# The recurrence's steps beside the token groups, interleaved four for three

## The chip, the cores and the metric

The kernel runs on one core of one Trainium2 chip. The metric is the device time of the program in microseconds. One execution on the chip was also taken with the hardware profiler; everything said of single instructions comes from it.

## The reference

One inference step of one decoder layer, for a prompt of 1024 positions and for 8 samples of 4 positions each, 1056 tokens in all, with 1024 features:

```
z = RMSNorm(x) @ W_in                                  # split between two head groups
h = x + [ RWKV7(z_rwkv) | MultiScalePool(z_pool) ] @ W_out
h = h + PEER(RMSNorm(h))                               # 8 heads: top 16 of 128x128 product keys, 16384 experts
h = h + (p @ W_ple) * sigmoid(RMSNorm(h) @ W_pg)
y = RMSNorm_final(h)
```

Two parts of it matter here. RWKV7 is a recurrence over the positions: a state of 64x64 for each of 8 heads goes from one position to the next, so it is done in order, here in chunks of 64 positions. PEER first projects the normalised h to queries (2048 columns), scores them against two sets of 128 keys, takes the best 16 of each, and the best 16 of their pairs; the experts so chosen are then applied.

## The kernel before

Products of 32-bit numbers are made as three matmuls of rounded halves (hi times hi, lo times hi, hi times lo: lines 677 to 679). Phase A projects x and prepares the recurrence's inputs. Then the tokens go through in four **groups** of 288, 256, 256 and 256 columns (`GROUPS`), and at the end a long dense part applies all experts to 672 of the tokens (line 1244), beside gathers for the others.

Between phase A and the dense part, three kinds of work run beside each other, each written as a Python generator that yields after each step:

- `b_stream` is the **recurrence**: 16 chunks of 64 positions (`bchunk`), up to three of them active, about 19 steps each. A chunk loads its inputs (`fdc`, line 504), makes a triangular inverse by six levels of small 64x64 matmuls (line 493) with ScalarE evacuations between them (lines 533 to 560), and then needs the state `S` of the chunk before (lines 580 to 618). Its tail normalises the output on VectorE (lines 625 to 639) and stores it to `y_d` (line 640).
- `phase_c` takes one **group** of 256 or 288 columns: it loads its part of `y_d` (line 720) and the residual `h` from `hx_d` (line 725), splits y (lines 708 and 709), applies W_out in eight blocks with a residual add each (line 739), norms, and makes 16 blocks of query projections (evacuated in line 800), whose weights come in 256 KB loads (lines 666 and 667, three buffers each). The scores of four heads' halves at a time go to `sc_d` (line 811). In between, the normed and split h is stored for the dense part; the last such store, `xl_d` (line 776), reads the tile h itself. The tile h has one buffer. The group's y needs the four chunks of 64 positions that it covers.
- `t_stream` picks the experts of the group before (`top`, `select`): score rows come from `sc_d` (line 833), then VectorE takes maxima and their places, five instructions to a score row (lines 836 to 841). For some tiles the gates are then spread by small matmuls (line 1025), built by VectorE from one-hot tiles (lines 1017 to 1019), evacuated by ScalarE (line 1026) and stored; for others GpSimd scatters them (line 965).

The program goes in **rounds** (the loop at line 1258). Round one runs group one beside chunks 5 to 7; round two runs group two beside chunks 8 to 11 and the experts of group one; round three runs group three beside chunks 12 to 15 and the experts of group two. (The first 128 tokens' experts are written ahead of round two, all at once.) Round four has no recurrence left: it runs group four beside the first blocks of the dense part. So each round's recurrence makes the y that the next round's group loads first.

`merge` sets the order in which the steps of a round are written: of the streams that still live, it takes a step of the one with the smallest share done, the number of steps taken divided by a length that was stated for the stream. The framework's scheduler then places each instruction on its engine's queue, by its own estimate of times; where several are ready, those written first go first. The queues are in order: an instruction that waits holds up all behind it on its engine. SP issues nearly all loads and stores.

The lines that state the recurrence's length and run the round:

```
    def b_len(ca, cb):
        return (cb - ca) * 19
```

Of the kernel before, what the change touches and what calls it, by code (L numbers as in the profile page):

```python
# [65 lines left out]
def body(ctx, tc, io):  # L66
# [977 lines left out]
    def b_stream(ca, cb, ahead=2):  # L1044
        while nxt[0] < cb or any(c < cb for c, _ in active):
            c = nxt[0]
            if (c < min(cb + ahead, NCH) and len(active) < NSLOT and (not active or since[0] >= STAG)
                    and not (held[0] and c % NSLOT == 1)):
                active.append((c, bchunk(c)))
                nxt[0], since[0] = c + 1, 0  # L1050
            since[0] += 1
            for a in list(active):
                try:
                    next(a[1])
                except StopIteration:
                    active.remove(a)
                yield

    def b_len(ca, cb):
        return (cb - ca) * 19  # L1060
# [6 lines left out]
    def t_stream(gi):  # L1067
        for t0, m in tiles_of(gi):
            if 0 < GROUPS[gi][0] + t0 < GB:
                yield from top(tk, GROUPS[gi][0] + t0, m)  # L1070

    def t_len(gi):
        n = 0
        for t0, m in tiles_of(gi):
            if 0 < GROUPS[gi][0] + t0 < GB:
                n += 24 + 16
        return n

    def merge(streams):
        live = [[0, n, g] for n, g in streams]  # L1080
        while live:
            s = min(live, key=lambda s: s[0] / s[1])
            try:
                next(s[2])
                s[0] += 1
            except StopIteration:
                live.remove(s)
# [164 lines left out]
    def upre():  # L1252
        for b in range(NPRE):
            ublock(b)
            yield

    CL = [0, 24, 24, 24, 24]
    for step in range(1, NG + 1):
        streams = []
        if step < NG:  # L1260
            c_ = BC[step + 2:step + 4]
            streams.append((b_len(*c_), b_stream(*c_)))
        if step == 2:
            for _ in top(tk, 0, 128):
                pass
        if 0 <= step - 2 < NG:
            streams.append((t_len(step - 2), t_stream(step - 2)))
        if 0 <= step - 1 < NG:
            streams.append((CL[step], phase_c(step - 1)))
        if step == NG:  # L1270
            for _ in streams[0][1]:
                pass
            gstack.close()
            late = ctx.enter_context(tc.tile_pool(name="late", bufs=1, side="right", reuse_waits="tile"))
            gqp = ctx.enter_context(tc.tile_pool(name="gqp", bufs=2, side="right", reuse_waits="tile"))
            streams = [streams[1], (NPRE, upre())]
        merge(streams)
        if step == NG - 1:
            nc.sync.dma_start(io["wkv_p"], S[-1])
            pbx.close()  # L1280
            dr = ctx.enter_context(tc.tile_pool(name="dr", bufs=1, side="right", reuse_waits="tile"))
            dps = ctx.enter_context(tc.tile_pool(name="dps", bufs=2, side="right", space=bass.MemoryType.PSUM, reuse_waits="tile"))
            XH, XL = xsplit()
            for k in range(KB):
                nc.sync.dma_start(XH[:, k, :].bitcast(F32), xh_d[:, k, :])
                nc.sync.dma_start(XL[:, k, :].bitcast(F32), xl_d[:, k, :])
            xs = [(XH[:, k, :], XL[:, k, :]) for k in range(KB)]
# [340 lines left out]
```

## Time and profile before

| what | value |
|---|---|
| median of 3 runs | 3213.11 us (3209.81 to 3214.63) |
| the profiled execution's own time | 3221.9 us |
| its span, first to last instruction | 3220.2 us |
| TensorE busy | 3048.1 us, 95% of the span |
| VectorE, ScalarE, GpSimd busy | 2554.8, 1058.8, 1702.7 us |
| mean granted TensorE clock | 0.972 |

The profile page gives each engine's busy time, the span in forty slices, the chain of work that ended last, and groups of instructions by source line. Further views of the same trace show any stretch: busy times by stretch, instructions in order of time, the chain of waits piece by piece. Engines are PE (TensorE; PEld its weight loads), DVE (VectorE), ACT (ScalarE), POOL (GpSimd) and SP (the queue that issues transfers). L739 is line 739 of the kernel.

### The profile page before, as it was taken

Reading aid. Unit: us, or ns where it says so; the run is one execution under the profiler, and the core shown is the slowest. Engines: PE = TensorE matmul, PEld = TensorE weight load, DVE = VectorE, ACT = ScalarE, POOL = GpSimd, SP = SyncE. Lnnn points to the kernel's source line nnn. Section 1 sums busy time; section 2 is a strip of 40 time slices with the busy share of each in tenths; the row PEclk is TensorE's granted clock in tenths of the full one; section 3 lists DMA queues with packets and bytes.
Section 4 is the critical chain, followed back from the end, with each engine's and each line's share of the span. In section 5 each row is a group of like instructions: output and inputs, shape, how many; then the busy total and the mean of one; then the engine's idle time right before and its main releaser. Section 6 shows DMA issues by size and latency. Waiting matters only on the chain.

```text
span 3220.2 us, 65859 instructions
## 1 busy us (share of the span) xinstructions
PE 3048.1 (95%) x26305; PEld 2945.9 (91%) x26305; DVE 2554.8 (79%) x5390; ACT 1058.8 (33%) x1636; POOL 1702.7 (53%) x1189
## 2 busy tenths in 40 slices
PE   8998899978888888999999999999999999999998
PEld 7887888967777788999999999999999999999998
DVE  7766445678497888988888888888888888888976
ACT  6452324433335545322222222212222212212253
POOL 5111410077887770066666656665666666666633
PEclk9999999988989899999999999999999999999999
DMA  5577457777868987389999999999999999999945
GB/s 172 155 201 184 119 165 241 264 190 167 217 143 218 332 230 244 116 316 344 326 340 353 321 339 344 330 332 357 328 323 350 332 331 340 341 329 341 332 135 185
DMA packets 462531, 863.33 MB, mean 268 GB/s; under 512 B 152848, under 2 KB 241168, under 8 KB 461840
## 3 DMA queue, kind: packets, MB, share of 16 engines
q1 hardware_dynamic: 305776, 436.32, 42.0%
q0 software_dynamic: 148128, 406.03, 37.4%
q10 hardware_dynamic: 8320, 16.78, 1.5%
q8 instruction: 206, 3.38, 0.4%
q14 instruction: 101, 0.83, 0.1%
HBM read 738.25 MB, written 120.73 MB: 267 GB/s over the span
## 4 chain that ended last, share of the span: by engine, by line
PE 78%; DVE 9%; DMA 8%; ACT 2%; issue 1%; SPq 1%; POOL 1%; ACTq 0%; DVEq 0%; POOLq 0%
PE pd L1244 59%; PE ps L493 5%; PE ps L231 3%; PE ps L677 2%; PE ps L679 2%; PE ps L678 2%; DMA scq<-sc_d 1%; DMA whi<-wc_d 1%; PE ps L1025 1%; PE ps L324 1%; DMA wlo<-wc_d 1%; PE ps L1147 1%; DMA sc_d<-scs 1%; DVE I L837 0%; DMA y_d<-yo 0%
## 5 line engine op out<-in xcount | busy, mean ns | idle before, releaser
L1364 POOL DMA_INDIRECT row<-u,idx x384 | 545.0, 1419 | 471.7 <-DMA eraw<-uT 149.1
L1364 POOL DMA_INDIRECT row<-v,idx x384 | 530.4, 1381 | 311.6 <-DVE po L1381 141.0
L1220 ACT ACTIVATE ehi<-eraw 128x1024 fp32r<-128x1024 f32 x278 | 294.8, 1060 | 1109.0 <-PE pd L1244 1038.2
L965 POOL DMA_INDIRECT gs<-gl,idx x256 | 436.2, 1704 | 258.5 <-DVE idx L958 137.9
L1244 PE MATMUL pd<-XL,ehi 128*128 128x336 f32 x2176 | 515.6, 317 | 0.0
L1244 PE MATMUL pd<-XH,elo 128*128 128x336 f32 x2176 | 514.1, 317 | 0.0
L1244 PE MATMUL pd<-XH,ehi 128*128 128x336 f32 x2176 | 510.7, 316 | 3.0 <-ACT OT L1250 2.8
L1244 PE MATMUL pd<-wh,ehi 128*128 128x336 f32 (+1 forms) x2112 | 502.9, 317 | 4.9 <-ACT wh L1314 4.7
L1244 PE MATMUL pd<-wl,ehi 128*128 128x336 f32 (+1 forms) x2112 | 503.8, 317 | 1.7 <-DVE wl L1316 1.7
L1244 PE MATMUL pd<-wh,elo 128*128 128x336 f32 (+1 forms) x2112 | 503.4, 317 | 0.0
L1381 DVE SCALAR_TENSOR_TENSOR po<-row,act,po 128x1024 f32<-128x1024 f32 x381 | 488.1, 1281 | 7.0 <-DVE act L1375 0.2
L1372 DVE SCALAR_TENSOR_TENSOR row<-row,xt 128x1024 f32<-128x1024 f32 x384 | 455.5, 1218 | 4.9 <-DMA xt<-xt_d 3.7
L1222 DVE TENSOR_TENSOR elo<-eraw,ehi 128x1024 fp32r<-128x1024 f32 x278 | 342.7, 1233 | 85.0 <-ACT ehi L1220 84.6
L1244 PEld LDWEIGHTS pd<-XH,ehi 128*128 128x128 f32 x2176 | 372.3, 189 | 3.9 <-ACT OT L1250 3.0
L1244 PEld LDWEIGHTS pd<-XH,elo 128*128 128x128 f32 x2176 | 372.6, 188 | 0.0
L1244 PEld LDWEIGHTS pd<-XL,ehi 128*128 128x128 f32 x2176 | 370.1, 188 | 0.0
L1244 PEld LDWEIGHTS pd<-wh,ehi 128*128 128x128 f32 x2112 | 362.2, 188 | 5.5 <-ACT wh L1314 5.0
L1244 PEld LDWEIGHTS pd<-wl,ehi 128*128 128x128 f32 x2112 | 362.1, 188 | 2.0 <-DVE wl L1316 2.0
L1244 PEld LDWEIGHTS pd<-wh,elo 128*128 128x128 f32 x2112 | 363.2, 188 | 0.0
L677 PE MATMUL ps<-hi,whi 128*128 128x256 f32 (+1 forms) x592 | 188.9, 320 | 45.5 <-DMA whi<-wc_d 26.8
L1324 DVE TENSOR_TENSOR OT<-pd,OT 128x672 f32<-128x672 f32 x120 | 102.8, 857 | 136.7 <-PE pd L1244 136.3
L679 PE MATMUL ps<-hi,wlo 128*128 128x256 f32 (+1 forms) x592 | 182.7, 309 | 6.6 <-DMA wlo<-wc_d 4.8
(461 smaller groups left out, 4885.3 us busy)
## 6 DMA issues: line engine op xcount, KB each, us to landing
eraw<-uT SPq DMA_DIRECT2D x128, 512.0 KB
eraw<-vP SPq DMA_DIRECT2D x128, 512.0 KB
whi<-wc_d SPq DMA_DIRECT2D x108, 256.0 KB
wlo<-wc_d SPq DMA_DIRECT2D x108, 256.0 KB
g_d<-gst SPq DMA_DIRECT2D x52, 512.0 KB
gq<-g_d SPq DMA_DIRECT2D x32, 832.0 KB
gs<-zero ACTq DMA_DIRECT2D x8, 2048.0 KB
gq<-gs SPq DMA_DIRECT2D x64, 256.0 KB
```

What stands on the lines that cost most here:

```text
L231: mm(ps[:, :XW], s[:, k, :], x[:, k, a:b], start=first, stop=last)
L493: mm(o[hs], l[hs], r[hs], start=start, stop=stop)
L677: mm(ps[:, :n], whi[:, kk, :], xhi, start=k == 0, stop=False)
L679: l = mm(ps[:, :n], wlo[:, kk, :], xhi, start=False, stop=k == K - 1)
L965: l = nc.gpsimd.indirect_dma_start(out=flat, out_offset=bass.IndirectOffsetOnAxis(ap=off[:, hh, k:k + 1], axis=0), in_=gl[:, hh, k:k + 1], ...
L1220: ACT(hi, raw, AF.Copy)
L1222: sub(lo, raw, hi.bitcast(F32), op=ALU.subtract)
L1244: mm(ps[:, a, :n], w_[:, k, :], x_[:, s:s + n], start=first, stop=last)
L1324: TT(halves(OT[db]), ps[:, :, :NH], halves(OT[db]), op=ALU.add)
L1364: nc.gpsimd.indirect_dma_start(out=r[:m], out_offset=None, in_=io[tab], in_offset=bass.IndirectOffsetOnAxis(ap=idx[:m, hh, k:k + 1], axis=0))
L1372: STT(r[:m], r[:m], 1.0, xt[:m], op0=ALU.mult, op1=ALU.mult, accum_out=pre[:m, k:k + 1])
L1381: STT(po[:m], r[:m], act[:m, k:k + 1], po[:m], op0=ALU.mult, op1=ALU.add)
```

## The change

The length that the recurrence states to `merge` is four thirds of what it was, in the three rounds that it shares with the groups:

```
         streams = []
         if step < NG:
             c_ = BC[step + 2:step + 4]
-            streams.append((b_len(*c_), b_stream(*c_)))
+            streams.append((b_len(*c_) * 4 // 3, b_stream(*c_)))
```

`merge` counts a stream's share as steps taken over the stated length. With the longer length each step of the recurrence counts three quarters as much, so four are written where three were, and the recurrence comes to its end when the other streams are at three quarters. No step is added or left out.

Three places show how the queues come out. The first is ScalarE at the border from round one to round two. L800 evacuates a query block of the old group, L708 splits y of the new one, L741 is the square after its first residual add, L810 evacuates scores, and the rest (`zp`, `yx`, `vt`, `wn`) belongs to the recurrence. Before, from after the last L800 on:

```order
L555 ACTIVATE kbT<-ps 128x512
L539 ACTIVATE zp<-ps 128x256
L560 ACTIVATE vt<-ps 128x256
L580 ACTIVATE wn<-ps 128x256
L810 ACTIVATE scs<-ps,rt 32x512
L547 ACTIVATE yx<-ps 128x512
L708 ACTIVATE hi<-gst 128x256 x4
L585 ACTIVATE zp<-ps 128x256
L539 ACTIVATE zp<-ps 128x256
L741 ACTIVATE sa<-h 128x256
```

Now, from the split on:

```order
L708 ACTIVATE hi<-gst 128x256 x4
L800 ACTIVATE q<-ps 128x288
L772 ACTIVATE xhi<-h 128x288
L585 ACTIVATE zp<-ps 128x256
L810 ACTIVATE scs<-ps,rt 128x512 x2
L539 ACTIVATE zp<-ps 128x256
L810 ACTIVATE scs<-ps,rt 32x512
L547 ACTIVATE yx<-ps 128x512
L741 ACTIVATE sa<-h 128x256
```

The split now stands ahead of the last L800, and of nine evacuations of the recurrence between the last L800 and L741 (two of them stand above the rows shown) three are left. At the border from round two to round three nine become four.

The second place is SP's queue at the same border: L640 stores the last y of the round, L720 loads y, L725 loads h, L833 loads scores. Before:

```order
L776 DMA xl_d<-h 1024x1x288
L640 DMA y_d<-yo 512x1x64
L504 DMA fdc<-fd 128x1792
L811 DMA sc_d<-scs 128x512 x2
L720 DMA gst<-y_d 128x4x256
L725 DMA h<-hx_d 128x256 x7
L833 DMA scq<-sc_d 128x512
```

Now the store and the load of y, and further down, with 24 rows of the queue between the two pieces, h:

```order
L640 DMA y_d<-yo 512x1x64
L504 DMA fdc<-fd 128x1792
L720 DMA gst<-y_d 128x4x256
L663 DMA wc_d<-whi 128x512 x2
L664 DMA wc_d<-wlo 128x512
```

```order
L776 DMA xl_d<-h 1024x1x288
L811 DMA sc_d<-scs 128x512 x2
L666 DMA whi<-wc_d 128x512
L667 DMA wlo<-wc_d 128x512
L725 DMA h<-hx_d 128x256 x2
L833 DMA scq<-sc_d 128x512 x2
```

The load of y is now ahead of the last projections' transfers, and between `xl_d` and the loads of h no wait for y is left.

The third place is VectorE in round two, just ahead of the group's eighth residual add (L739). Names with V and s hold score rows, SC and cand the pairs picked from them, and L187 is the reciprocal in a chunk's tail. Before:

```order
L840 MAX V_8132<-s_8235 128x8
L841 MAX_INDEX I_8133<-V_8132,s_8214 128x8
L943 TENSOR_REDUCE gl_7803<-oh 128x32 x2
L955 ISA ci<-ci,r_8031 128x128
L841 MAX_INDEX I_8133<-V_8132,s_8235 128x8
L839 MATCH_REPLACE s_8278<-V_8132,scq 128x128
L836 MAX V_8132<-scq 128x8 x4
L739 TENSOR_TENSOR h<-ps,h 128x256
```

Now:

```order
L891 MATCH_REPLACE cand<-SC,s_8510 128x50
L187 RECIPROCAL s_9023<-s_9023 128x4
L890 MAX_INDEX CI<-SC,s_8551 128x8
L891 MATCH_REPLACE cand<-SC,s_8551 128x50
L912 TENSOR_TENSOR gt<-SC 128x64
L739 TENSOR_TENSOR h<-ps,h 128x256
```

Before, the score rows of the tile V_8132 were still under way when the add came; now the pairs of these rows are being picked, and a chunk's tail stands among them. From the round's first residual add to its eighth, VectorE's queue held 12 starts of a score row (L836) before and holds 20 now.

More of the change, by code (lines that the diff above doesn't have):

```diff
@@ L1261, in body @@
             c_ = BC[step + 2:step + 4]
-            streams.append((b_len(*c_), b_stream(*c_)))
+            streams.append((b_len(*c_) * 4 // 3, b_stream(*c_)))
         if step == 2:
```

## The prediction, as it was put on record

> **What bounds the kernel now.** I read the busy times of the rounds first, then the chain of waits around their borders, then the two engines there in order of time. In the first two views the columns are: stretch, its length, busy us of PE, PEld, DVE, ACT and POOL (instructions in brackets), granted TensorE clock, DMA share, GB/s.
>
> ```profile
> 502.36:662.81 160.45, 150.84 (x2478) 140.67 (x2474) 98.24 (x361) 73.78 (x160) 17.16 (x11) 0.97 0.80 267
> 662.81:863.11 200.30, 162.38 (x2536) 149.70 (x2538) 140.40 (x777) 66.81 (x147) 153.88 (x97) 0.88 0.78 184
> 863.11:1069.90 206.79, 163.16 (x2282) 149.41 (x2277) 167.13 (x752) 86.78 (x160) 166.84 (x98) 0.88 0.83 201
> 1069.90:1298.00 228.10, 198.51 (x1543) 188.86 (x1542) 197.01 (x748) 121.58 (x165) 99.80 (x53) 0.90 0.88 256
> 1298.00:3079.00 1781.00, 1780.95 (x11608) 1780.88 (x11609) 1561.97 (x2212) 441.58 (x525) 1079.74 (x770) 1.00 0.90 325
> ```
>
> From 1298 us on TensorE has no gap, and the change doesn't touch that part. So the end moves only by what TensorE's idle time before 1298 loses or gains: 9.6 us in round one, 37.9 in round two, 43.6 in round three. In round one TensorE is the limit (94%). Inside rounds two and three the limit changes from slice to slice:
>
> ```profile
> 720.00:740.00 20.00, 13.51 (x181) 12.51 (x179) 19.70 (x123) 4.01 (x10) 16.96 (x11) 0.83 0.41 54
> 760.00:780.00 20.00, 17.20 (x229) 15.58 (x229) 16.64 (x93) 3.53 (x9) 16.95 (x11) 0.83 0.87 222
> 820.00:840.00 20.00, 15.87 (x260) 14.38 (x256) 10.13 (x42) 7.79 (x12) 16.95 (x11) 0.97 0.88 204
> 840.00:860.00 20.00, 19.66 (x274) 17.73 (x274) 3.82 (x16) 6.58 (x16) 16.65 (x12) 0.86 0.92 229
> 860.00:880.00 20.00, 12.80 (x198) 11.95 (x198) 9.27 (x43) 3.91 (x11) 16.65 (x12) 0.83 0.92 228
> 880.00:900.00 20.00, 14.82 (x303) 13.25 (x303) 20.00 (x136) 7.50 (x20) 16.95 (x11) 1.00 0.80 172
> 1020.00:1040.00 20.00, 16.95 (x224) 15.64 (x221) 12.83 (x38) 10.81 (x16) 16.95 (x11) 0.92 0.95 224
> ```
>
> Early in rounds two and three VectorE is full (19.70 and 20.00 of 20) and TensorE waits; late in them VectorE is light (3.82 to 12.83) and TensorE and the transfers are the limit; at the border (860 to 880) nobody is full. The chain of waits names what stands there (start, length, what):
>
> ```profile
> 653.72 9.07 DMA y_d<-yo
> 662.81 5.86 DMA gst<-y_d
> 668.68 3.69 DMA scq<-sc_d
> ...
> 857.36 5.69 DMA y_d<-yo
> 863.11 6.78 DMA gst<-y_d
> ```
>
> The last chunk of a round stores its rows of y, and the next group loads them back: 14.9 us at the first border, 12.5 at the second. In order of time on SP's queue, TensorE and VectorE (start, length, engine, line; in brackets the idle time before and what ended it):
>
> ```profile
> 653.00 0.62 SPq L776 DMA_DIRECT2D xl_d<-h  x1
> 662.81 0.57 SPq L720 DMA_DIRECT2D gst<-y_d  x1
> 663.47 0.62 SPq L725 DMA_DIRECT2D h<-hx_d  x1
> 854.61 0.53 SPq L776 DMA_DIRECT2D xl_d<-h  x1
> 863.78 0.64 SPq L725 DMA_DIRECT2D h<-hx_d  x1
> 649.24 0.29 PE L679 MATMUL ps<-hi,wlo 128*128 128x288 f32 x1
> 667.72 1.12 PE L493 MATMUL ps<-yx,ltm 64*64 64x64 f32 x16 [7.24 <-ACT yx L547]
> 870.38 0.80 PE L677 MATMUL ps<-hi,whi 128*128 128x256 f32 x2 [6.17 <-ACT hi L708]
> 676.57 0.40 DVE L739 TENSOR_TENSOR h<-ps,h 128x256 f32<-128x256 f32 x1
> 878.08 0.40 DVE L739 TENSOR_TENSOR h<-ps,h 128x256 f32<-128x256 f32 x1
> ```
>
> SP's queue is in order: until the load of y may start at 662.81, the loads of h and of the scores behind it wait too. From the group's last projection matmul (649.24) to the next group's first residual add (676.57) pass 27 us.
>
> **The change part by part.** No instruction's kind or count changes; steps change places. In the new order (shown above) y's load is issued during the projections, its split (L708) stands ahead of the last evacuation of q, and h's loads wait for something else: the store of xl_d, which reads h's only buffer.
>
> Border one. The store is issued at 653.00 and done issuing at 653.62. Its landing has no row. Near ones are 3.69 us (a small load) and 9.07 us (the store of y issued right behind it on the same busy engines); I take 6, nearer the middle since it is larger than the one and ahead of the other: 659.6. Then h's load: 0.62 to issue and the 3.69 of the score load: the first add at 663.9, 12.7 us sooner than 676.57. Against that stands what filled the wait. This view has L493, the recurrence's matmuls, alone (busy us of PE and PEld; clock; DMA), for both borders:
>
> ```profile
> 649.53:669.50 19.97, 9.40 (x252) 8.38 (x252) 0.88 1.08 303
> 852.30:870.38 18.08, 9.02 (x268) 8.23 (x268) 0.97 1.08 287
> ```
>
> ScalarE's order has nine evacuations of the recurrence in the first gap before and three now, so six ninths of 9.40, 6.3 us, go ahead into round one, where TensorE is 94% full, and are paid for in full. Net 6.4 us; with a landing of 9.07 it is 3.3, with 3.69 it is 8.7.
>
> Border two. 854.61 + 0.53 + 6 = 861.1; plus 0.64 and 3.69 is 865.5, against 878.08: 12.6 us. Nine evacuations become four, so five ninths of 9.02, 5.0 us, go ahead into slices where TensorE is busy 35.5 of 40 us: 4.4 paid. Net 8.2, between 5.1 and 10.5. Both borders: 14.6 us (8.4 to 19.2).
>
> A rule of the Trainium skill bears here: "TensorE: Matmul & The Clock Gate", the section on the HAM clock gate, says that after about 3.4 us without work the array falls to half its clock, and needs about 3.4 us of work to recover. The gaps of 7.24 and 6.17 us are long enough, so by it each costs a cold start of 1.7 us, and their going would give 3.4 us more than my sum. The trace agrees only in part: the slice 860 to 880 has 0.83, but 720 to 740 has 0.83 as well.
>
> The stages between. What runs earlier in a round meets the full VectorE. In the stage of round two that applies W_out (from the first residual add, L739, to the eighth) VectorE's order now holds 20 score rows (one L836 each) instead of 12, and one more tail of a chunk is begun. A score row costs five instructions, from this grouping (line, engine, operation, count; busy us, mean ns; idle before):
>
> ```profile
> L841 DVE FIND_INDEX8 I<-V,s 128x8 uint32<-128x128 f32 x116 | 32.3, 282 | 0.0
> L837 DVE FIND_INDEX8 I<-V,scq 128x8 uint32<-128x128 f32 x116 | 31.7, 283 | 0.0
> L839 DVE MATCH_REPLACE8 s<-V,scq 128x128 f32<-128x128 f32 x116 | 31.6, 274 | 0.0
> L840 DVE MAX8 V<-s 128x8 f32<-128x128 f32 x116 | 30.5, 280 | 0.0
> L836 DVE MAX8 V<-scq 128x8 f32<-128x128 f32 x118 | 26.8, 278 | 47.3 <-DMA scq<-sc_d 47.2
> L1017 DVE TENSOR_TENSOR ab<-iota,e 128x2048 f16<-128x2048 f16 x52 | 62.9, 1216 | 20.5 <-PE ps L1025 17.2 <-ACT e L1003 3.0
> L1018 DVE TENSOR_TENSOR ab<-ab,e 128x1024 f16<-128x1024 f16 x52 | 35.1, 680 | 0.3
> L513 DVE TENSOR_TENSOR ltm<-ps,nmt 128x768 f32<-128x768 f32 x18 | 16.3, 949 | 13.5 <-PE ps L493 13.5
> L627 DVE SCALAR_TENSOR_TENSOR zp<-s,ps 128x256 f32<-128x256 f32 x12 | 4.9, 410 | 0.2
> L1026 ACT ACTIVATE gst<-ps 128x512 f32<-128x512 f32 x104 | 104.9, 1119 | 56.7 <-PE ps L1025 56.0 <-issue 0.4
> ```
>
> That is 1.4 us; eight are 11.2, and with two L513 (1.9) and half of a chunk's tail (eight steps like L627 at 0.41, 3.3 whole) 15 us, all on the path at 19.70 of 20. The projections behind it have eight score rows fewer, where VectorE has 16.64 of 20: it gives back 83%, 12.5. Loss 2.5 us. Round three: in the first half of its projections stand two chunk tails more (6.6), one state update (0.8) and two sets of one-hot tiles for the gates (L1017 and two like L1018, 2.6 each: 5.2), 12.6 us, and its W_out stage has one tail and one update less, 4.1: 8.5 us more at a full VectorE. The second half gives it back, at 12.83 of 20, so 64%: loss 3.1. If nothing were given back both cost 23.5, if all of it nothing.
>
> Border three isn't held by y. The fourth group finds eight more of the gate evacuations done at its first residual add (72 against 64); they alternate with the projections there. At 1.12 us each (L1026) that is between nothing and 9 us; I take 3, as TensorE has other work beside it.
>
> Sum: 14.6 - 5.6 + 3 = 12 us off the profiled execution, whose own time was 3221.9 us (span 3220.2), 8.8 above the median of the runs. 3213.1 - 12 gives 3201 us.
>
> **The rivals.** *Nothing to be measured*: h's store and loads take y's place in full (landing 9 us, both borders 8.4), and the stages take 5.6: 3 us, 3210. For it: the transfers have a share of 1.08 in both gaps. For it too: the order moves the recurrence less than the words say; at the last query block of round one ScalarE has 148 of its evacuations behind it for 141 before, of some fifty in a round. Against: the store of y is ahead of that traffic now. *Slower*: VectorE in round two's W_out stage and the first half of round three's projections. If the late slices don't get shorter, because weights and TensorE set them (DMA 0.92 and 0.95), 23.5 us are added and 14.6 saved: 3222 with border three unchanged. It decides once less than 8.9 of the 23.5, 38%, is given back. For it: 20.00 of 20 there. Against: TensorE is busy 19.66 in 840 to 860, and part of that is the recurrence. *More*: all 27.4 us of the four chain pieces go, and the work that goes ahead finds idle time: with border three 3183. Against: round one has only 9.6 us idle. *The clock*: without the recurrence between them the late projections leave gaps at every wait for weights, and TensorE is granted less: 0.83 for 0.97 in the last 40 us of rounds two and three is 11 us, so 3212. That is the mechanism of the clock gate's page, turned against the change; the rows bear it out weakly, as 0.97 stands beside 15.87 us of work.
>
> **How the numbers follow.** Forecast 0.43, with its own range of 3191 to 3210 (sum with the borders' bounds and the gate term); nothing 0.13; slower 0.25; more 0.13; clock 0.06. A measurement of this kernel tells about 0.2%, 6.4 us, from no change. Faster than 3206.7 is 0.37 of the forecast's 0.43, and more: 0.50. Within: 0.06 + 0.13 + 0.06 = 0.25. Slower: 0.25. The range goes from 3178, which takes in most of *more*, to 3226, past the price of *slower*.
>
> **What would show it.** Borders right: no y_d store or y load in the chain of waits there, the first residual add 12 to 14 us behind the last projection's matmul instead of 27, and h's loads right behind xl_d. Wrong: y still waited for, or 20 us and more. Stages right: rounds two and three, from first add to first add, within 10 us of 201.5 between the two adds above; wrong if one is 15 longer with VectorE full. The clock: under 0.85 in the last 40 us of a round. The forecast fails if the stages lose more than the borders give, or if TensorE's idle time before its unbroken run hardly falls.

## The result: 0.7% slower

| | median | lowest to highest | runs |
|---|---|---|---|
| before | 3212.81 us | 3209.81 to 3214.63 | 4 |
| after | 3235.59 us | 3230.11 to 3237.35 | 4 |

The ratio is 1.0069, with a 95% interval of 1.0055 to 1.0083: slower by 0.7%, 22 us, where 3201 us had been forecast; the range ended at 3226.

The page of the changed kernel, its first part, and two slices of 20 us early in round three (stretch, length, busy us of PE, PEld, DVE, ACT and POOL with instructions in brackets, granted TensorE clock, DMA share, GB/s):

```profile
span 3235.6 us, 65871 instructions
...
PE 3045.0 (94%) x26305; PEld 2943.6 (91%) x26305; DVE 2552.5 (79%) x5390; ACT 1056.4 (33%) x1634; POOL 1712.8 (53%) x1189
...
900.00:920.00 20.00, 13.68 (x252) 12.86 (x252) 20.00 (x129) 9.74 (x23) 16.66 (x12) 0.66 0.40 55
920.00:940.00 20.00, 10.60 (x88) 9.57 (x86) 19.80 (x107) 3.54 (x9) 17.26 (x10) 0.74 0.51 110
```

TensorE, VectorE and ScalarE have no more work than before. What grew is the time in which TensorE does nothing: early in round three, while VectorE is full, and at the end of round four. In the same slices of the kernel before TensorE was busy 16.93 and 16.17 us and VectorE 20.00 and 17.07.

At the two borders the queues do what was foretold. SP's queue and the first residual adds after the change, in order of time (start, length, engine, line; in brackets the idle time before and what ended it):

```profile
662.25 0.53 SPq L776 DMA_DIRECT2D xl_d<-h  x1
671.44 1.14 SPq L725 DMA_DIRECT2D h<-hx_d  x2
674.37 0.81 DVE L739 TENSOR_TENSOR h<-ps,h 128x256 f32<-128x256 f32 x2 [3.56 <-DMA h<-hx_d]
861.55 0.54 SPq L776 DMA_DIRECT2D xl_d<-h  x1
868.19 4.17 SPq L725 DMA_DIRECT2D h<-hx_d  x7
872.66 0.76 DVE L739 TENSOR_TENSOR h<-ps,h 128x256 f32<-128x256 f32 x2 [2.72 <-DMA h<-hx_d]
```

The load of y isn't among them any more; h's loads stand right behind the store of xl_d. To see where the time went instead, I cut both traces at the same events: the first residual add of each group (L739), the last projection evacuation of a group (L800), in round two also the last residual add, in round three also the fourth projection evacuation, and the 90 us behind the fourth group's last. Same columns, before:

```profile
517.71:649.57 131.86, 127.01 (x1897) 118.27 (x1896) 88.83 (x331) 62.65 (x134) 4.52 (x3) 0.97 0.78 271
649.57:676.57 27.00, 17.84 (x340) 16.08 (x340) 9.13 (x38) 7.81 (x18) 20.55 (x14) 0.87 1.02 276
676.57:709.99 33.42, 24.81 (x432) 23.14 (x432) 31.30 (x188) 12.02 (x27) 25.91 (x16) 0.88 0.75 170
709.99:853.41 143.42, 120.96 (x1776) 111.41 (x1778) 101.99 (x556) 46.48 (x101) 110.62 (x69) 0.88 0.75 174
853.41:878.08 24.67, 17.73 (x332) 16.37 (x332) 8.62 (x34) 7.15 (x17) 20.43 (x14) 0.86 1.00 253
878.08:948.72 70.64, 58.10 (x911) 53.14 (x913) 67.68 (x406) 25.31 (x62) 59.34 (x38) 0.86 0.67 136
948.72:1102.51 153.79, 122.87 (x1474) 111.48 (x1473) 118.63 (x354) 79.11 (x115) 118.36 (x65) 0.86 0.96 259
1102.51:1260.00 157.49, 144.02 (x1194) 138.84 (x1191) 141.21 (x614) 87.76 (x121) 76.42 (x41) 0.96 0.85 233
1260.00:1350.00 90.00, 80.12 (x490) 79.06 (x491) 80.40 (x393) 27.54 (x36) 0.00 (x0) 0.94 0.52 168
```

and after:

```profile
518.47:659.96 141.49, 133.53 (x2102) 124.65 (x2101) 91.06 (x337) 66.39 (x145) 14.86 (x10) 0.98 0.80 270
659.96:674.37 14.41, 11.83 (x200) 10.78 (x200) 4.56 (x8) 3.96 (x8) 10.54 (x7) 1.00 1.10 293
674.37:726.22 51.85, 35.80 (x636) 32.34 (x632) 50.03 (x322) 15.88 (x35) 41.49 (x26) 0.80 0.67 151
726.22:859.77 133.55, 118.29 (x1836) 109.86 (x1838) 91.21 (x456) 48.62 (x107) 105.33 (x66) 0.91 0.80 193
859.77:872.66 12.89, 10.47 (x190) 9.53 (x190) 3.07 (x15) 4.11 (x9) 8.49 (x6) 1.00 1.07 281
872.66:955.78 83.12, 62.38 (x1025) 57.30 (x1026) 78.33 (x451) 29.06 (x70) 70.33 (x43) 0.84 0.61 129
955.78:1114.01 158.23, 122.77 (x1263) 111.98 (x1261) 114.14 (x326) 80.28 (x110) 121.44 (x66) 0.86 0.99 270
1114.01:1258.60 144.59, 131.95 (x1073) 127.30 (x1072) 129.35 (x585) 74.08 (x107) 64.25 (x36) 0.98 0.84 231
1258.60:1348.60 90.00, 68.02 (x420) 65.83 (x418) 87.11 (x431) 29.59 (x38) 2.52 (x3) 0.87 0.50 157
```

Length less PE busy gives TensorE's idle time of each stretch:

| stretch | length, before and after | TensorE idle, before and after | idle, difference |
|---|---|---|---|
| round one to its last projection | 131.9, 141.5 | 4.9, 8.0 | +3.1 |
| border one | 27.0, 14.4 | 9.2, 2.6 | -6.6 |
| round two, W_out stage | 33.4, 51.9 | 8.6, 16.1 | +7.4 |
| round two, the rest | 143.4, 133.6 | 22.5, 15.3 | -7.2 |
| border two | 24.7, 12.9 | 6.9, 2.4 | -4.5 |
| round three to the fourth projection block | 70.6, 83.1 | 12.5, 20.7 | +8.2 |
| round three, the rest | 153.8, 158.2 | 30.9, 35.5 | +4.5 |
| round four to its last projection | 157.5, 144.6 | 13.5, 12.6 | -0.8 |
| the 90 us behind it | 90, 90 | 9.9, 22.0 | +12.1 |

These add up to +16.2 us, and the spans differ by 15.4 (3235.6 and 3220.2). Idle time is the better account here: round four got shorter mostly because TensorE had less work in it (1073 matmuls for 1194), and what was left for later is done later.

These stretches hide one thing: the fourth block is a quarter of the projections. Cut at the last residual add, the eighth projection evacuation and the last one, the first and the second half of round three's projections were, before:

```profile
909.72:987.08 77.36, 67.66 (x962) 61.59 (x964) 71.00 (x347) 34.41 (x65) 62.67 (x36) 0.87 0.71 158
987.08:1063.41 76.33, 58.28 (x692) 54.14 (x693) 51.69 (x159) 31.31 (x49) 59.64 (x35) 0.84 0.95 243
```

and after:

```profile
901.50:1007.20 105.70, 80.81 (x1196) 74.23 (x1197) 98.13 (x484) 42.76 (x78) 88.04 (x49) 0.82 0.64 143
1007.20:1081.63 74.43, 57.36 (x503) 52.20 (x501) 53.54 (x125) 39.58 (x53) 56.10 (x31) 0.85 1.06 297
```

The first half grew by 28.3 us, 15.2 of them idle time of TensorE. The W_out stage ahead of it (31.6 to 28.8 us), the second half and border three (39.1 to 32.4) all got shorter, but their idle time fell by only 0.7, 1.0 and 0.8 us. Three groups of VectorE's instructions in the first half, before and then after (line, engine, operation, count; busy us, mean ns; idle before):

```profile
L1017 DVE TENSOR_TENSOR ab<-iota,e 128x2048 f16<-128x2048 f16 x9 | 10.8, 1209 | 0.0
L939 DVE TENSOR_TENSOR oh<-oh,gt 128x512 f32<-128x512 f32 x4 | 2.6, 675 | 0.0
L899 DVE MAX8 K<-s 128x8 f32<-128x50 f32 x8 | 1.3, 198 | 0.0
```

```profile
L1017 DVE TENSOR_TENSOR ab<-iota,e 128x2048 f16<-128x2048 f16 x11 | 13.2, 1209 | 0.0
L939 DVE TENSOR_TENSOR oh<-oh,gt 128x512 f32<-128x512 f32 x8 | 5.2, 678 | 0.0
L899 DVE MAX8 K<-s 128x8 f32<-128x50 f32 x16 | 2.7, 202 | 0.0
```

L1017 builds one-hot tiles for the gates, L939 is one of the comparisons that find the chosen experts (L938 to L943), and L899 takes a maximum over the pairs (the steps of lines 854 to 917).

One caution on the profiled execution of before. Three kernels below that keep its order through round three had 218.6 to 219.4 us there, where its own trace has 224.4; up to the fourth block TensorE was granted a clock of 0.86 in it and of 0.95 in those three. Its own time is 9 us above the median as well. By length round three's price is then 22 us or more (241.3 to 245.0 in four traces with the full change's order), by TensorE's idle time 13 to 17 (56.2 to 59.4 us, for 42.4 to 43.5 in the four traces with the order of before).

### The profile page after: what moved, and what is told of

It reads as the page before. It is cut to its first block, busy times and chain, and to the rows that moved or that the text cites. A ratio compares the mean times of both kernels' runs of the same rounds, so it can differ in the third digit from the quotient of the medians.

```text
span 3235.6 us, 65871 instructions
## 1 busy us (share of the span) xinstructions
PE 3045.0 (94%) x26305; PEld 2943.6 (91%) x26305; DVE 2552.5 (79%) x5390; ACT 1056.4 (33%) x1634; POOL 1712.8 (53%) x1189
## 3 DMA queue, kind: packets, MB, share of 16 engines
q1 hardware_dynamic: 305776, 436.32, 41.6%
## 4 chain that ended last, share of the span: by engine, by line
PE 65%; DVE 7%; DMA 5%; ACT 2%; issue 1%; SPq 1%; DVEq 0%; ACTq 0%
PE pd L1244 59%; PE ps L493 1%; DMA whi<-wc_d 1%; PE ps L677 1%; PE ps L679 1%; PE ps L678 1%; DMA scq<-sc_d 1%; PE ps L1025 1%; DMA wlo<-wc_d 1%; ACT gst L1026 1%; DMA sc_d<-scs 1%; PE ps L807 1%; DMA xl_d<-h 0%; DVE I L837 0%; DVE I L841 0%
## 5 line engine op out<-in xcount | busy, mean ns | idle before, releaser
L1364 POOL DMA_INDIRECT row<-v,idx x384 | 538.2, 1401 | 312.1 <-DVE po L1381 157.0
```

Source lines behind the costliest of these rows:

```text
L1364: nc.gpsimd.indirect_dma_start(out=r[:m], out_offset=None, in_=io[tab], in_offset=bass.IndirectOffsetOnAxis(ap=idx[:m, hh, k:k + 1], axis=0))
```

## The experiments

Four ideas were tested. **A**: gate evacuations (L1026) that were pulled ahead among round three's projections. **B**: gate evacuations left behind the last projection, which hold up the first load of gates. **C**: vector work of the recurrence put ahead into the stretches behind a border, where VectorE is full. And the wait at border three. On B, the expectations count gates by a listing that lost a few; the rows give 6 left behind the last projection evacuation in the full change, where two expectations have 13, and none before. Unless it says otherwise, a diff is against the changed kernel. Times are medians; each ratio is to the kernel before on the same chip (medians 3213.0 to 3215.7), and differences in us are taken from the ratios, 1% being 32 us.

### One round at a time

```
-            streams.append((b_len(*c_) * 4 // 3, b_stream(*c_)))
+            streams.append((b_len(*c_) * (4 if step == 1 else 3) // 3, b_stream(*c_)))
```

and the same with `step == 2`, `step == 3` and `step < 3`.

> Four for three in round one alone. Theory A (the loss is made in round three, where gate evacuations L1026 are pulled ahead between the last projections; this order has 53 of them ahead of the 48th projection for 43 before and 58 with the full change): slower, about 3222. Theory B (the loss is made at the end of round four: gate evacuations left over after the last projection hold up the first gate load; 100 of 104 are ahead of it here, 98 with the full change): slower, about 3220, with the wait after the last projection and not at the 48th. Theory C (vector work put ahead into the W_out stages of rounds two and three): nothing beyond the 2 us that border one gains, 3211.

> Four for three in round two alone. Theory A: nothing (43 gate evacuations ahead of the 48th projection, as before), 3208 to 3213. Theory B: slower, about 3220 (100 of 104 ahead of the last projection). Theory C: slower by the W_out stage's 18 us less what the projections give back, about 3222.

> Four for three in round three alone. Theory A: slower, about 3225 (52 ahead of the 48th projection, 72 for 64 at the fourth group's first add). Theory B: nothing, 3210 to 3216 (all 104 ahead of the last projection). Theory C: slower by about 8, 3221.

> Four for three in rounds one and two, round three as before. Theory A and theory B: the two borders' gain is left, 2 to 5 us, 3208 (40 ahead of the 48th projection, 104 ahead of the last). Theory C: slower, 3228 or more, since both W_out stages with more vector work ahead are still there.

| four for three in | time | ratio, 95% interval | first add of group one to that of group three |
|---|---|---|---|
| round one | 3209.96 us | 0.9993 (0.9983 to 1.0002) | 344 us |
| round two | 3231.77 us | 1.0053 (1.0035 to 1.0071) | 376 us |
| round three | 3214.63 us | 1.0007 (0.9995 to 1.0020) | 360 us |
| rounds one and two | 3195.89 us | 0.9949 (0.9932 to 0.9965) | 354 us |
| all three | 3235.59 us | 1.0069 (1.0055 to 1.0083) | 354 us |
| none (before) | 3212.81 us | 1 | 360 us |

The rounds don't add up: -2, +17 and +2 us alone, -16 for the first two, +22 for all. **Four for three in rounds one and two alone beats both kernels.** It differs from the full change by round three's number only, and that number costs 39 us, though alone it costs nothing. So neither borders nor stages can be priced one by one. No theory fits the four results: round one alone came out as C had it and round three alone as B had it, while round two alone is 10 us above the highest forecast and the first two rounds 12 us below the lowest.

### What the last gates cost (B)

The same edit in both kernels; the last 32 tokens' gates are left out:

```
+            cut = col == 544 and t1 == m - TC
+            if not cut:
+                st = gp.tile([128, EB, TC], F32, name="gst", bufs=2)
-            for t2 in range(0, TC, GT8):
+            for t2 in range(0, 0 if cut else TC, GT8):
```

> The kernel before with the last 32 tokens' gates left out (their one-hot tiles, 32 small matmuls and 8 evacuations are not made; the chunk before is stored in their place, so these tokens' output is wrong). No gate evacuation is left behind the last projection. Theory B (what is left behind it holds up the dense part): TensorE's 9.9 us idle after the last projection mostly go, 3203 to 3207. Theory A: 3210 to 3213, only the work left out.

> The changed kernel with the same 32 tokens' gates left out in the same way; the order up to group four's 60th projection is that of the changed kernel. Theory B: the 22 us idle after the last projection fall to a few, so that it is 6 to 12 us slower than the kernel before with the same cut, where the whole change was 22 slower. Theory A (all is lost by the fourth group's first add): the distance stays at 18 to 22.

Measured: 3204.8 us (0.9975, 0.9965 to 0.9984) and 3219.58 us (1.0024, 1.0012 to 1.0036). The distance falls from 22 us to 16. Idle behind the last projection fell in both kernels (to 1.2 and 10.3 us), so 9 of the 12 us of difference there stayed. Taken with round four's own idle time (18.9 and 14.2 us), the difference is 4.4 us where it was 11.2. So the pair takes a part of the end's loss away, but not cleanly.

### Other ratios in round three

```
-            streams.append((b_len(*c_) * 4 // 3, b_stream(*c_)))
+            streams.append((b_len(*c_) * (4/3, 4/3, 7/6)[step - 1], b_stream(*c_)))
```

and `5 // 3`, `(4/3, 4/3, 5/6)`, `(4/3, 1, 3/4)`, `(5/3, 5/3, 1)` in its place.

> Four for three in rounds one and two, seven for six in round three. The order has 40 gate evacuations ahead of the 48th projection (as in the good kernel with rounds one and two alone) and 96 of 104 ahead of the last (the changed kernel: 98). Theory A: as rounds one and two alone, 3196 to 3200, with the fourth group's first add near 1070. Theory B: that first add near 1070 too, but 12 us or more idle after the last projection, 3206 to 3212.

> Five for three in all three rounds. The order has 54 gate evacuations ahead of the 48th projection and all 104 ahead of the last. Theory A: round three as slow as with the full change (first add of group four at 1105 to 1115), 3225 or more. Theory B: no idle time at the end, 3210 to 3218, whatever round three takes. If neither counts and earlier y is simply better: 3190.

> Four for three in rounds one and two, five for six in round three, so that there the recurrence ends later than its round's other work and gates come later still: 40 gate evacuations ahead of the last but eight of round three's projections (55 in the full change, 39 with the ratio one), and all 104 ahead of the last projection's evacuation. Theories A and B both ask for no loss here: rounds three and four take 361 us or less as with the ratio one, and TensorE's idle time behind the last projection is near nothing: 3190 to 3198 us. If instead what matters in round three is that the recurrence ends with the round (the store of y and its load return at border three): 3203 to 3210.

> Four for three in round one alone, one in round two, three for four in round three. By the sums so far round one's edit is worth 16 us in rounds one and two (344 us for 360), and round three's slower recurrence leaves the gates late: 38 ahead of the last but eight of round three's projections, all 104 ahead of the last projection's. Theory A with B: rounds three and four take 361 to 373 us, and the end has no idle time: 3180 to 3195 us, less than any so far. If effects don't add because what is put off comes back in the next round (the first group-four stage has 70 gates behind it and VectorE full): 3200 to 3210.

> Five for three in rounds one and two, one in round three. In the run with five for three throughout rounds one and two took 348 us (first residual add to first residual add) for 354 with four for three; round three had 54 gates ahead of its last projections there and takes 202 to 217 us with the ratio one. By the order 40 gates stand ahead of round three's last projection here, and 52 ahead of the fourth group's first stage for 64 before; four are left behind the last projection. Theory A: 3188 to 3198 us, at least as good as four for three in two rounds (3196). If what is put off into round four comes back there: 3203 to 3210.

| ratios | time | ratio, 95% interval | round three | TensorE idle in it |
|---|---|---|---|---|
| 4/3, 4/3, 7/6 | 3214.72 us | 1.0004 (0.9992 to 1.0015) | 216.7 us | 41.6 us |
| 5/3, 5/3, 5/3 | 3211.33 us | 0.9995 (0.9985 to 1.0006) | 237.5 us | 55.1 us |
| 4/3, 4/3, 5/6 | 3204.76 us | 0.9970 (0.9956 to 0.9984) | 204.4 us | 42.4 us |
| 4/3, 1, 3/4 | 3218.80 us | 1.0010 (0.9998 to 1.0022) | 241.4 us | 56.8 us |
| 5/3, 5/3, 1 | 3203.68 us | 0.9972 (0.9959 to 0.9984) | 199.4 us | 37.6 us |
| 4/3, 4/3, 1 (above) | 3195.89 us | 0.9949 (0.9932 to 0.9965) | 201.6 us | 30.8 us |

Behind rounds one and two at 4/3, round three is best at the old ratio: with 5/6 7 us are lost, with 7/6 18, with 4/3 39. With 3/4 the recurrence is late at border three: its last y is stored at 1063 us, 46 us behind the group's last projection evacuation. Going on to 5/3 in the first two rounds saves some 7 us there by the trace (346 us from the first group's first add to the third's, for 354), but that doesn't carry to the end. The expectations for 3/4 (3180 to 3195) and for 5/3, 5/3, 1 (3188 to 3198) were wrong, and 5/6 came out at its second forecast (3203 to 3210). Theory A also missed with 5/3 throughout (3225 or more) and with 7/6 (3196 to 3200): there just as few gates stand ahead of round three's last projection as in the best kernel, 40, and 18 us are lost all the same. B missed 7/6 too, by 3 us.

### Round three's gates put late, with the faster recurrence (A)

```
-            streams.append((t_len(step - 2), t_stream(step - 2)))
+            streams.append((t_len(step - 2) * (1/2 if step == 3 else 1), t_stream(step - 2)))
```

> The full change, but in round three the list that holds the first tile's experts and gates is stated half as long, so that its steps are put behind those of the projections instead of evenly among them. In the new order ScalarE has 42 gate evacuations (L1026) ahead of the last but eight of round three's projections' evacuations where the full change has 58, and 98 of 104 ahead of the last. Theory A (the loss comes from gate work pulled ahead between round three's projections, where VectorE was full): round three falls from 241 us (first residual add to first residual add) to 225 or less, and with fewer gates left at the end the time is about 3215 us, at most 3222. Theory B alone (the loss is the gates left behind the last projection, which hold up the first load of gates): six left instead of 13 saves some 8 us, 3228, with round three unchanged. Neither: 3235.

Measured: 3221.38 us, 1.0017 (1.0007 to 1.0026), so 17 us under the full change (14 by the medians). The trace: round three's W_out stage, the first and the second half of its projections, round four, and the 90 us behind:

```profile
867.49:897.87 30.38, 23.91 (x382) 21.49 (x382) 24.31 (x137) 10.40 (x27) 25.43 (x17) 0.89 0.85 186
897.87:982.40 84.53, 66.29 (x1047) 60.21 (x1048) 80.39 (x464) 25.58 (x61) 67.13 (x42) 0.86 0.61 122
982.40:1052.19 69.79, 55.17 (x525) 50.70 (x524) 54.58 (x123) 42.14 (x54) 50.61 (x28) 0.90 1.11 323
1086.03:1241.74 155.71, 141.75 (x1168) 135.85 (x1167) 136.66 (x586) 84.41 (x118) 83.21 (x48) 0.93 0.86 235
1241.74:1331.74 90.00, 67.92 (x411) 65.05 (x411) 81.60 (x377) 29.79 (x38) 0.00 (x0) 0.85 0.52 164
```

The first half falls from 105.7 us to 84.5, with VectorE's work in it from 98.1 to 80.4. What left it is the gates: none of their evacuations is made there now, where the full change has 18 and the kernel before 14, while the steps on pairs (217 instructions) and the comparisons (24 for 23) stay. All of it comes from the fifth to the eighth block; up to the fourth the time stays long (86.3 us). The second half, with 34 gates for 32, got shorter too (69.8 us for 74.4). So in this pair gates hurt in the first half, and not in the second. The 22 us behind the last projection stay, though the round before was mended.

### The same gates put early, with the old recurrence

Against the kernel before:

```
-            streams.append((t_len(step - 2), t_stream(step - 2)))
+            streams.append((t_len(step - 2) * (7/6 if step == 3 else 1), t_stream(step - 2)))
```

> The kernel before, the recurrence's ratio one in all rounds, but in round three the list that holds the first tile's experts and gates is stated a sixth longer: by the order 50 gate evacuations stand ahead of the last but sixteen of all projection evacuations (the last of round three) where the kernel before has 43, 72 ahead of the fourth group's first stage for 64, and all 104 ahead of the last projection's in both. Theory A (gates ahead of round three's projections cost, whatever the recurrence does): half of what the full change puts ahead, so half of the 14 to 22 us that its gates cost, 3221 to 3226, with round three 230 us or more for 219 to 224. If they cost only together with the faster recurrence, which fills VectorE in the same slices: 3214, within 5, with round three unchanged.

Measured: 3207.02 us, 0.9975 (0.9965 to 0.9984): 8 us faster. Theory A as it stood falls. Round three did get longer, but its idle time did not, and round four and the end have less:

```profile
879.04:950.31 71.27, 57.48 (x926) 51.68 (x926) 69.65 (x375) 27.37 (x65) 60.01 (x38) 0.93 0.65 135
950.31:1111.94 161.63, 132.97 (x1544) 120.11 (x1544) 134.40 (x501) 85.14 (x120) 120.26 (x65) 0.86 0.99 265
1111.94:1261.88 149.94, 136.22 (x1102) 130.85 (x1101) 126.42 (x503) 81.65 (x115) 75.77 (x42) 0.97 0.87 246
1261.88:1351.88 90.00, 89.31 (x586) 88.96 (x585) 89.75 (x466) 30.96 (x40) 5.02 (x4) 1.00 0.49 165
```

The first half of round three's projections has 18 gates here, as in the full change, but took 76.7 us, with VectorE busy for 72.8. So more gates there don't cost by themselves, and that they do behind a faster recurrence rests on the run with gates put late.

### The wait at border three

In the full change the first vector instruction on scores stands 12.35 us at border three while SP's queue issues the loads of XH and XL. The edit writes these loads behind the last tile's experts:

```
         if step == NG:
             for _ in streams[0][1]:
                 pass
+            for k in range(KB):
+                nc.sync.dma_start(XH[:, k, :].bitcast(F32), xh_d[:, k, :])
+                nc.sync.dma_start(XL[:, k, :].bitcast(F32), xl_d[:, k, :])
```

(and takes the same three lines out of the step before).

> The full change, but the loads of the last blocks' normalized rows for the experts (XH and XL) are written behind the fourth group's first tile's experts and not ahead of them. In the full change the fourth group's first vector instruction on the scores stands still for 12.35 us at border three while SP's queue issues these loads ahead of the score load (1097.98 to 1104.24). If that wait is on the path, round three gets 6 to 10 us shorter and the time is 3225 to 3229. If other work fills it or the loads only collide later: 3235, within 5. The order has 100 of 104 gate evacuations ahead of the last projection's instead of 91, so theory B asks for 8 us of its own, seen as TensorE idle time behind 1250 us falling from 22 to 8: by it the time is 3227 with round three unchanged, and with both 3219.

Measured: 3227.79 us, 1.0040 (1.0026 to 1.0054), 9 us under the full change, but not for the reason given: the wait is still 9.7 us, and round three was 245.0 us for 241.3. The end's idle time fell to 17.3 us, and the trace is 6 us shorter in rounds one and two, whose order this edit doesn't move (nine traces with that order have 348 to 355 us there). What the 9 us are stays open.

### What is left behind the last projection, by itself (B)

One number at the place where round four is merged: 3 in the full change, 1.25 and, as the control, 3 in the kernel before, and 3 in the half-length kernel above:

```
-            streams = [streams[1], (NPRE, upre())]
+            streams = [streams[1], (NPRE*3, upre())]
```

> The full change, but in round four the list of the eight first expert blocks is stated three times as long against the fourth group's stages, which brings them sooner and, by the new order, all 104 gate evacuations ahead of the last projection's evacuation on ScalarE (98 in the full change). Nothing before round four moves. Theory B (what is left behind the last projection costs by itself): TensorE's idle time in the 90 us behind the last projection falls from 22 us to 2 to 9, as in every kernel so far that has none left, and the time by 8 to 12 us to 3224 to 3228. Theory A alone: 3235, what is saved at the end being lost in round four. Round three stays at 241 us by both.

> The kernel before with the list of the eight first expert blocks stated a quarter longer, and no other edit: by the order it leaves six gate evacuations behind the last projection's evacuation, as many as the full change, where the kernel before leaves none. Theory B: the idle time behind the last projection rises from 9.9 us to 17 to 22 and the time by 8 to 12 us to 3222 to 3227. Theory A alone: 3214, no change.

> The kernel before with the list of the eight first expert blocks stated three times as long: the control for the edit in full_up3. None of the gates is left behind the last projection, as in the kernel before. If the edit has no price of its own the time is that of the kernel before, 3214 within 5; what it differs by is to be taken off the result of full_up3.

> The full change with both edits: round three's experts stated half as long (fewer gates among its projections, 14 us in the earlier run) and round four's first expert blocks three times as long (no gate left behind the last projection). If A and B are the whole loss and stand apart, the two savings add up: 3221 less 8 to 12 is 3209 to 3213, some 24 us under the full change and level with the kernel before, or up to 8 us below it if the borders' gain shows. If B is none of it: 3221.

| kernel | time | ratio, 95% interval | idle in round three | in round four | behind it |
|---|---|---|---|---|---|
| before, 1.25 | 3216.09 us | 0.9998 (0.9985 to 1.0011) | 43.3 | 11.4 | 15.0 |
| before, 3 | 3229.02 us | 1.0045 (1.0031 to 1.0059) | 42.4 | 32.3 | 0.0 |
| full change, 3 | 3238.61 us | 1.0074 (1.0052 to 1.0096) | 59.4 | 30.6 | 0.0 |
| half-length experts, 3 | 3216.13 us | 1.0004 (0.9995 to 1.0014) | 45.6 | 23.7 | 3.3 |

Theory B comes out both ways. Against it: six gates left behind in the kernel before cost nothing that can be measured (0.9998), and the full change without any left didn't get faster: the end's 22 us went into round four, which has 30.6 for 12.6. For it: the number 3 costs the kernel before 14 us, and the expectation of that control had said that this is to be taken off. So taken, the full change gains 13 us, where B asked for 8 to 12. Idle time moves freely between round four and the end, so only their sum says anything: 23.4 us before and 34.6 after, but 32.3 and 30.6 with the number 3, where no excess is left. With the number 3 the full change stands 9 us above its control, and the half-length kernel 13 below it. So putting round three's gates late is worth 17 us in one pair and 22 in the other. Where the end's 11 us come from isn't settled.

### What the first stretch of round three follows (C)

Each kernel's order says how many of the recurrence's ScalarE evacuations (L533 to L585) stand between the third group's first residual add and its fourth projection block. Beside it the time between these two events:

| evacuations ahead | time to the fourth block, us |
|---|---|
| 15 | 54.6 (4/3, 1, 3/4), 58.8 (5/3, 5/3, 1) |
| 16 | 55.4 (4/3, 4/3, 5/6) |
| 18 | 58.0 (rounds one and two) |
| 19 | 63.9 (round two alone) |
| 22 | 70.6 (before), 65.4 and 65.5 (before with 1.25 and 3), 71.3 (gates early), 69.2 (round one alone), 60.1 (4/3, 4/3, 7/6) |
| 28 | 83.1 (full), 86.3 (half-length), 82.4 (late loads), 83.3 and 85.9 (both with 3) |
| 30 | 84.9 (5/3) |
| 32 | 89.0 (round three alone) |

From 15 to 32 the time grows by some 32 us, 1.9 us for each, but at the count of 22 alone it lies between 60.1 and 71.3 us, so the count isn't all of it. Four for three in rounds one and two *alone* brings the count down from 22 to 18, since more of the recurrence is done at the third group's first add (212 of its evacuations for 208); four for three in round three brings it up to 28 or 32. The chain of waits between the last residual add and the fourth block, after the change, is VectorE nearly throughout (50.7 of 54.3 us); these are its longest pieces between 914 and 920 us (start, length, what):

```profile
914.72 1.20 DVE oh L938 x2
916.52 1.19 DVE oh L939 x2
918.63 1.19 DVE gl L943 x2
```

and before, where at the same distance from the round's start transfers and TensorE have come in:

```profile
921.40 4.49 DMA xt_d<-xt
925.97 0.69 ACT xt L792
927.10 4.64 DMA whi<-wc_d
931.78 0.58 PE ps L677
```

From the fifth to the eighth block the chain names TensorE for 29.9 us of 51.4, transfers for 13.1 and VectorE for 8.3, so there VectorE's work is one load among others.

In the kernel that beats both, the first half of the projections (first row) is 41 us shorter than in the full change, and the second half much the same:

```profile
892.04:956.35 64.31, 60.35 (x838) 54.02 (x835) 64.28 (x326) 29.31 (x59) 55.47 (x30) 0.92 0.75 174
956.35:1029.84 73.49, 57.95 (x703) 52.53 (x704) 63.54 (x251) 33.52 (x53) 54.57 (x31) 0.91 0.99 258
```

By TensorE's idle time, 21 of the 36 us between these two traces (from the first add to the unbroken run) stand in this half, and 13 in round four and behind it. The half's length goes with VectorE's busy time in it: 64.3 us with 64.3 busy here, 77.4 with 71.0 before, 84.5 with 80.4 with half-length experts, 84.8 with 76.8 with seven for six, 99.2 with 84.9 with round three alone, and 105.7 with 98.1 in the full change. The steps on pairs in it are 130 here and 217 in the full change. Why they fall there in the one order and not in the other isn't shown.

A long first half isn't always paid for. With four for three in round three alone it was 99.2 us, but the W_out stage was 6.3 us and border three 8.6 us shorter than before, idle time at the end was low (18.2 us with round four's), and the whole came out level.

## Why the prediction was wrong

**Right in this pair: what sets the end.** The time moves by what TensorE's idle time ahead of its unbroken run loses or gains. The difference of 16.2 us of idle time stands for 15.4 of span. Between other kernels the rule is rougher, since TensorE's busy time for the same instructions also varies: from 3036.0 us (rounds one and two) to 3053.5 (round two alone).

**Right: the mechanism at the borders.** From last projection evacuation to first add the borders went from 27.0 and 24.7 us to 14.4 and 12.9: 12.6 and 11.8 sooner, for 12.7 and 12.6 foretold. The loads of h begin 8.7 us behind the end of xl_d's issue at border one, near the upper bound, and 6.1 at border two, for 6.

**Too large in part: what the borders are worth.** TensorE's work in the two gaps fell from 17.8 and 17.7 us to 11.8 and 10.5. So 6.0 and 7.3 us of work were moved out, where 6.3 and 5.0 were foretold. In idle time border one gave 6.6 us for 6.4 and border two 4.5 for 8.2, 11.1 for 14.6 together. Round one took back 3.1 besides: it grew by 9.6 us where 6.3 were foretold.

On the clock, border rows bear out part of a rule. TensorE's granted clock was 0.87 and 0.86 in the two borders before, which had its waits of 7.24 and 6.17 us, and 1.00 in both after. On 17.8 us of work at 0.87 that is 2.3 us a border, by estimate. The Trainium skill, "TensorE: Matmul & The Clock Gate", in its section on the HAM clock gate, says that the array drops to half its clock after an idle window of about 3.4 us; by its figures the prediction estimated 1.7 us a border. The trace agrees in direction and about in size. It didn't decide anything in this pair: over the whole of round two the clock went from 0.88 to 0.89 and of round three from 0.86 to 0.85. In the first half of round three's projections it fell from 0.87 to 0.82; no run separates that from the idle time beside it.

**Off by size, evened out: round two.** Its W_out stage grew by 18.4 us for 15 foretold, and its projections gave back 9.9, 54% and not 83%. In idle time the two even out (+7.4 and -7.2).

**The step that failed: round three's term of 12.6 us for "the first half of its projections", and behind it "the second half gives it back, at 12.83 of 20, so 64%: loss 3.1".** The first half grew by 28.3 us, and VectorE's work in it by 27.1. What the prediction had counted is there: two chunk tails and two sets of one-hot tiles more. It had left out the experts' other steps, which the same order moves into this half: those on pairs go from 141 to 217 instructions and the comparisons from 12 to 23, some 15 us of VectorE's time. Its W_out stage gave 2.8 us for 4.1 foretold. So 25.5 us stand where 8.5 were put down.

The second half then gave back 1.9 us, 1.0 in idle time. VectorE had no less work in it (53.5 us for 51.7), and 32 gates are evacuated there instead of 21. The eight gates more ahead of the fourth group's first add, put down as a gain of 3 us at border three, go with a border 6.7 us shorter, but only 0.8 of that was idle time. In idle time round three lost 12.7 us in the pair where 3.1 were foretold. With the gates taken out of the first half, it is 84.5 us instead of 105.7 and the kernel 17 us faster; with the old ratio in round three it is 64.3, and the kernel 39 us faster.

**The rival that came out.** "Slower" named VectorE in round two's W_out stage and the first half of round three's projections, and priced it at 3222, if nothing is given back. The place was right and the size was not: it had 8.5 us for round three, where 25.5 were measured. The end's 11 us, which no case held, came on top. So the range stopped below the result. "The clock" found no support in the form it had: in the last 40 us ahead of the first adds of groups three and four the clock was 0.91 and 0.87, not under 0.85. "More", at 3183, is what four for three in the first two rounds came nearest to, 3196.

**Open.** The end's share: 11.2 us more of idle time in round four and behind it. Gates left behind the last projection are neither shown as its cause nor excluded: in the kernel before six of them cost nothing, but with the same edit to round four in both kernels the excess is gone, and with the last gates left out of both it is 4.4 us. Open too is why four for three in round two alone costs 17 us, though the first half of round three's projections is short there (74.1 us).

## What to carry to other kernels

Where several streams of work are interleaved in fixed proportions, a stage that was to "give back" time must be looked at for what else the same edit puts there: count, in the new order, every kind of work between each milestone and the next, not only the kind that was moved. Here the recurrence's tails and the gates' tiles were counted, and the experts' steps on pairs and their comparisons were not. Price a shortened wait by the idle time in it and not by its length, since work that filled it has to go elsewhere. And try the proportions one stage at a time: the best setting tried here (four for three in the first two of three rounds, 0.5% faster) lies between two that are worse, and no round's effect could be told from that of the others.
